# An encoder of two layers in exact fp32 halves: another order of the products in the FFN's second down-projection, and one weight load ordered behind rotary swaps

## The chip, the cores and the metric

The kernel runs on one core of a Trainium2 chip. The metric is the device time of one execution in microseconds (us), the median of several runs. The engines are named as the profile names them: PE is TensorE (matmuls; PEld its weight loads), DVE is VectorE, ACT is ScalarE, POOL is GpSimd, and SP is SyncE, which here issues DMAs and nothing else. "SPq" is SP's queue.

## The reference

Two layers of an encoder over 512 tokens of width 1024, all in fp32:

```python
for i in range(DEPTH):                       # 2 layers
    h = rmsnorm(x, norm_mix[i])
    qa, ka, va, glu_in, qc, kc, vc, gates = split(h @ w_in[i])
    ya = diff_attention(qa, ka, va, ...)     # 4 heads, q and k rotated (rope)
    yb = conformer_conv(glu_in, ...)         # 31 taps, depthwise
    yc = neighbourhood_attention(qc, kc, vc, rpb[i])
    ga, gb, gc = split(sigmoid(gates))
    x = x + (ga*(ya @ w_br_a) + gb*(yb @ w_br_b) + gc*(yc @ w_br_c)) @ w_o[i]
    h = rmsnorm(x, norm_ffn[i])
    x = x + (silu(h @ w_ffn_gate[i]) * (h @ w_ffn_up[i])) @ w_ffn_down[i]   # 1024 -> 2816 -> 1024
    h = rmsnorm(x, norm_ple[i])
    x = x + sigmoid(h @ w_ple_gate[i]) * (p[i] @ w_ple_in[i])
return rmsnorm(x, norm_final)
```

The rotation of q and k is `x * cos + rot * sin`, where `rot` holds the two halves of each head's 64 rows exchanged.

## The kernel before

**Halves.** Every fp32 operand of a product is split into a high half, which ACT writes (a Copy into fp32r, L150), and a low half, which DVE writes (the operand less the high half, L164). Each product of 128 rows is then three matmuls: high by high, high by low, low by high. The loader `weights` (from L172) loads a weight block of up to 128x1024 on SP (L178) into one of three buffers `wr` and splits it into `wh` (ACT) and `wl` (DVE), of which there are three each too. Loads and splits get a higher priority, so that the scheduler places them ahead of the place where the program writes them.

**Who orders what.** PE executes in the order in which the program is written. On ACT, DVE, POOL and SP a scheduler sets the order of instructions by priorities and by what they wait for, before the program runs. An explicit edge without a wait, `behind(i, then)`, tells that scheduler to place `i` behind `then`.

**Differential heads.** `diff_in` (from L836) does one head: for q and then for k a projection (whose weight load is that of `weights`), a copy of the result to `rp`, four swaps of 32 rows each from one `rp` buffer to another by DMA on SP (L852, "rotary swaps"), then on DVE the two products with the tables, their sum and the split, and four or more DMAs that stack the halves (L670). In the profile a swap is `diff_rp<-diff_rp`, the products with the tables end in `diff_rp<-diff_rp,diff_r`, and the names' numbers tell tiles apart: `diff_rp_1483` is filled by the swaps of k of head 0, and `diff_wr_1930` is the weight load of q of head 2. The neighbourhood attention (`natten_...`) and the convolution (`conv_...`) of the same layer run among this work; `diff_mm` at L185 is the first matmul of the next projection.

**FFN.** Its 22 blocks of 128 hidden rows are done in three parts, of 8, 7 and 7 blocks. Within a part `seven` (from L1126) does gate and up of a block with seven products instead of eight, in the manner of Strassen (L1168 to L1170). After the first and the second part `seven_down` (from L1024) adds what the part's hidden rows give to the output, for four pairs p = 0 to 3 of output blocks of 128 rows. A pair takes seven products R0, R1, T0, T1, A0, A1, C0, and the whole-weight products M and N for the part's last chunk:

```python
steps = dict(R0=(R, 0, "a11", "b11"), R1=(R, 1, "s2", "t1"), T0=(T, 0, "s3", "t2"),
             T1=(T, 1, "s1", "t3"), A0=(A, 0, "a12", "b21"), A1=(A, 1, "s4", "b22"),
             C0=(C, 0, "a22", "t4"))
```

Each step names its PSUM tile and half, its weight operand and its activation operand. A product is 9 matmuls of 128x256 (L1068 to L1070); M and N together are the matmuls of 128x512 (L1079 to L1081). The weight operands a11, a12, m0 come from one load; s1, s2, m1 are sums, which the DMAs form as they land in a `qk` tile (loads on SP at L1033 to L1035, added to by POOL's DMAs at L1039); the third and the fourth sum are made by DVE from the others: s3 = s1 + a22, s4 = s3 + a12. Then the two pairs of sums are split: ffn_wh and ffn_wl hold s1, s2, m1; ffn_y (pair 2) or ffn_pt (pair 3) hold both halves of s3 and s4. So DVE's last work for a pair before PE can take T0's low half is the `TENSOR_TENSOR` to ffn_y or ffn_pt. When R0 and R1 are done, ACT copies R; when R and T are complete, DVE takes four subtractions and then the two additions whose results go out by DMA on SP (L1121, `xa`).

The order in which a pair's steps stand in the program is a string. It differs by pair and by `last`, which is 1 in the second part. In the second part, pair 1 has T0 seventh of nine steps (M and N are steps here), pair 2 third and pair 3 second. In pair 2 R and T are the `sc` tiles of PSUM and A is `av`; in pair 3 R and T are the `tr` tiles and A and C `mm`. After pair 3 of the second part comes the third part's first block, whose loads for the blocks ahead (L1133 to L1138) are among the pair's own on SP.

## Time and profile before

| | us |
| --- | --- |
| median of 3 runs | 1765.66 |
| lowest and highest run | 1763.92, 1765.74 |
| the profiled execution | 1766.5 |
| its span, first to last instruction | 1764.7 |
| PE busy in the span | 1753.3 (99%) |
| DVE busy | 1474.0 (84%) |
| ACT busy | 929.3 (53%) |
| POOL busy | 140.3 (8%) |

The profile lists for each engine the instructions with their start and length. An idle time before an instruction stands in square brackets, followed by what ended it: "[0.88 <-DVE ffn_y L164]" is 0.88 us in which the engine waited for a DVE instruction of line 164 that wrote ffn_y. The granted TensorE clock over the profiled execution was 0.999 of full speed. PE's records are shown longer than the distance between two of their starts, because matmuls are pipelined; lengths of stages are therefore read from start to start. In all there are 10578 matmuls in the trace.

### The profile page before, as it was taken

What the parts mean: (1) busy time and instruction counts of PE and PEld (TensorE: products, weight loads), DVE (VectorE), ACT (ScalarE), POOL (GpSimd) and SP (SyncE); (2) the same over time, 40 slices, a digit from 0 to 9 for tenths busy, and PEclk for the clock granted to TensorE, in tenths of its full rate; (3) what the DMA queues carried; (4) which work ended last, traced back from release to release, by engine and by line L of the source; (5) the groups of instructions that cost most, each with busy time, mean ns of one, the idle gap of its engine ahead of it and who ended that gap; (6) DMA issues with size and microseconds to landing.
All of it is one profiled execution on the core that took longest, in us unless ns stands there. A gap on an engine that the chain in (4) does not pass through costs nothing.

```text
span 1764.7 us, 28718 instructions
## 1 busy us (share of the span) xinstructions
PE 1753.3 (99%) x10578; PEld 1565.9 (89%) x10578; DVE 1474.0 (84%) x2528; ACT 929.3 (53%) x1623; POOL 140.3 (8%) x162
## 2 busy tenths in 40 slices
PE   9999999999999999999999999999999999999998
PEld 7888888888899999998888888888888999999987
DVE  7967987998799889887777678889887997988786
ACT  5576545225576455454545655553356654545454
POOL 0000000000111111210000000000001121212100
PEclk9999999999999999999999999999999999999999
DMA  6576641334867777975546755323358668679642
GB/s 225 164 185 160 162 126 44 112 99 140 264 166 174 203 195 174 252 195 164 164 134 172 183 150 152 111 72 96 97 178 241 177 167 223 175 197 241 160 153 95
DMA packets 137901, 288.67 MB, mean 164 GB/s; under 512 B 17184, under 2 KB 38432, under 8 KB 137760
## 3 DMA queue, kind: packets, MB, share of 16 engines
q1 hardware_dynamic: 117456, 251.96, 46.7%
q0 software_dynamic: 19584, 33.56, 11.9%
q8 instruction: 83, 1.36, 0.3%
q10 hardware_dynamic: 720, 1.31, 0.2%
q14 instruction: 58, 0.48, 0.1%
HBM read 236.43 MB, written 19.92 MB: 145 GB/s over the span
## 4 chain that ended last, share of the span: by engine, by line
PE 90%; DVE 5%; ACT 3%; DMA 1%; issue 1%; SPq 0%; POOLq 0%; DVEq 0%; ACTq 0%
PE ffn_mm L1168 4%; PE ffn_mm L1170 4%; PE ffn_mm L1169 4%; PE ffn_sc L1168 3%; PE ffn_sc L1170 3%; PE ffn_sc L1169 3%; PE mergea_mm L187 2%; PE mergea_mm L186 2%; PE mergea_mm L185 2%; PE gateb_mm L186 2%; PE gateb_mm L187 2%; PE wo_mm L186 2%; PE wo_mm L185 2%; PE gateb_mm L185 2%; PE wo_mm L187 2%; PE diff_sc L834 2%
## 5 line engine op out<-in xcount | busy, mean ns | idle before, releaser
L167 DVE SCALAR_TENSOR_TENSOR conv_z<-glu_z,pre_par,conv_z 128x512 f32<-128x512 f32 x240 | 179.4, 748 | 3.4
L1138 POOL DMA_DIRECT2D ffn_qk<-w_fu x88 | 77.7, 964 | 437.3 <-DMA ffn_qk<-w_fu 131.5
L164 DVE TENSOR_TENSOR ffn_wl<-ffn_wr,ffn_wh 128x1024 fp32r<-128x1024 f32 (+1 forms) x76 | 89.3, 1177 | 6.7 <-ACT ffn_wh L150 6.7
L150 ACT ACTIVATE ffn_wh<-ffn_qk 128x1024 fp32r<-128x1024 f32 (+1 forms) x60 | 62.7, 1046 | 49.5 <-PE ffn_mm L1081 14.6
L150 ACT ACTIVATE ffn_wh<-ffn_wr 128x1024 fp32r<-128x1024 f32 (+1 forms) x76 | 76.9, 1014 | 22.5 <-PE ffn_mm L186 12.0
L164 DVE TENSOR_TENSOR ffn_wl<-ffn_qk,ffn_wh 128x1024 fp32r<-128x1024 f32 (+1 forms) x60 | 72.3, 1205 | 8.2 <-ACT ffn_wh L150 7.9
L150 ACT ACTIVATE mergea_wh<-mergea_wr 128x1024 fp32r<-128x1024 f32 (+1 forms) x32 | 27.1, 846 | 96.8 <-PE mergea_mm L186 79.6
L150 ACT ACTIVATE ffn_kh<-ffn_r 128x512 fp32r<-128x512 f32 (+1 forms) x60 | 35.9, 598 | 39.4 <-PE ffn_mm L1169 19.9
L231 POOL TENSOR_TENSOR diff_rc<-diff_sm,pre_power 128x4 f32<-128x4 f32 x8 | 8.9, 1116 | 564.4 <-DVE diff_sm L167 505.9
L150 ACT ACTIVATE natten_e<-natten_e,natten_s 128x192 f32<-128x192 f32 (+1 forms) x88 | 39.3, 473 | 26.2 <-DVE natten_s L732 22.9
L150 ACT ACTIVATE diff_a<-diff_sc,diff_s 128x512 f32<-128x512 f32 x32 | 22.0, 686 | 56.7 <-DVE diff_s L925 56.6
L1168 PE MATMUL ffn_sc<-wo_h,ffn_wh 128*128 128x256 f32 x176 | 50.4, 287 | 0.2 <-ACT ffn_t L150 0.2
L1169 PE MATMUL ffn_mm<-wo_h,ffn_wh 128*128 128x256 f32 x176 | 49.8, 283 | 0.0
L1170 PE MATMUL ffn_mm<-wo_h,ffn_wl 128*128 128x256 f32 x176 | 49.8, 283 | 0.0
L1168 PE MATMUL ffn_mm<-wo_h,ffn_wh 128*128 128x256 f32 x176 | 49.8, 283 | 0.0
L1170 PE MATMUL ffn_sc<-wo_h,ffn_wl 128*128 128x256 f32 x176 | 49.8, 283 | 0.0
L1169 PE MATMUL ffn_sc<-wo_h,ffn_wh 128*128 128x256 f32 x176 | 49.8, 283 | 0.0
L164 DVE TENSOR_TENSOR diff_wl<-diff_wr,diff_wh 128x1024 fp32r<-128x1024 f32 x24 | 29.4, 1223 | 18.6 <-ACT diff_wh L150 13.6
L150 ACT ACTIVATE natten_wh<-natten_wr 128x1024 fp32r<-128x1024 f32 x24 | 25.4, 1058 | 36.7 <-issue 15.2
L925 DVE TENSOR_REDUCE diff_s<-diff_sc 128x1 f32<-128x512 f32 x64 | 42.0, 682 | 2.2 <-PE diff_sc L834 2.1
L164 DVE TENSOR_TENSOR natten_wl<-natten_wr,natten_wh 128x1024 fp32r<-128x1024 f32 x24 | 29.3, 1222 | 12.4 <-ACT natten_wh L150 10.4
L164 DVE TENSOR_TENSOR ffn_qk<-ffn_qk,ffn_r 128x512 f32<-128x512 f32 (+1 forms) x60 | 38.8, 647 | 0.0
(1082 smaller groups left out, 6980.2 us busy)
## 6 DMA issues: line engine op xcount, KB each, us to landing
ffn_qk<-w_fu POOLq DMA_DIRECT2D x88, 256.0 KB, 6.2
ffn_wr<-w_fg SPq DMA_DIRECT2D x44, 512.0 KB, 5.6
ffn_r<-w_fu SPq DMA_DIRECT2D x44, 256.0 KB, 3.7
ffn_qk<-w_fg SPq DMA_DIRECT2D x44, 256.0 KB, 4.7
ffn_qk<-w_fu SPq DMA_DIRECT2D x44, 256.0 KB, 5.1
ffn_wr<-w_fd SPq DMA_DIRECT2D x24, 448.0 KB, 4.2
natten_wr<-w_in SPq DMA_DIRECT2D x16, 512.0 KB, 4.6
diff_wr<-w_in SPq DMA_DIRECT2D x16, 512.0 KB, 4.2
```

The lines of the kernel that those rows point to most:

```text
L150: i = self.nc.scalar.activation(out, in_, func, **kw)
L164: return self.nc.vector.tensor_tensor(out, a, b, op)
L167: return self.nc.vector.scalar_tensor_tensor(out, a, s, b, op0, op1)
L185: mm(out, wh, ah, start=first, stop=False, skip_group_check=onto)
L186: mm(out, wh, al, start=False, stop=False, skip_group_check=onto)
L187: mm(out, wl, ah, start=False, stop=last, skip_group_check=onto)
L834: self.nc.tensor.matmul(out, st4[:, u, qs], st[:, ks], start=n == 0, stop=n == 1)
L925: nc.vector.tensor_reduce(out=m[:, u:u + 1], in_=sc, op=ALU.max, axis=AX.X, negate=True)
L1138: nc.gpsimd.dma_start(q, wu[:, lo], accum_op=ALU.add)
L1168: mm(out, wh[:, c], bh, start=first and k == 0, stop=False, skip_group_check=True)
L1169: mm(out, wh[:, c], bl, start=False, stop=False, skip_group_check=True)
L1170: mm(out, wl[:, c], bh, start=False, stop=k == 3, skip_group_check=True)
```

## The change

Two edits. The first is one condition and one string, in the order of the steps in the second part's down-projection: pair 2's order string is changed and now holds for pair 3 too, which had the default order. Within it the products of the third sum (T0) and of the fourth sum (A1) stand fifth and eighth of nine; before, T0 was third in pair 2 and second in pair 3, and A1 was eighth in both. The second edit adds an ordering edge on SP: the weight load of head 2's q (`s` = 0) is placed behind the last swap of head 0's k.

```diff
@@ weights
-            self.nc.sync.dma_start(raw[:, :n], ap[:, :n])
+            load = self.nc.sync.dma_start(raw[:, :n], ap[:, :n])
+            if self.hold is not None:
+                self.behind(load, self.hold)
@@ build
+        self.hold = None
@@ diff_in
         for s, off in enumerate((OFF_QA, OFF_KA)):
+            self.hold = self.swap if (head, s) == (2, 0) else None
             ps = self.proj(off + head * P)
             ...
             for b in range(4):
                 o = b ^ 1
-                self.nc.sync.dma_start(rot[32 * b:32 * b + 32], raw[32 * o:32 * o + 32])
+                swap = self.nc.sync.dma_start(rot[32 * b:32 * b + 32], raw[32 * o:32 * o + 32])
             ...
+        if head == 0:
+            self.swap = swap
@@ seven_down
         order = "R0 T0 R1 T1 A0 M N A1 C0"
         ...
-        elif last and p == 2:
-            order = "R0 A0 T0 R1 T1 M N A1 C0"
+        elif last:
+            order = "R0 A0 R1 T1 T0 M N A1 C0"
```

Line numbers of the changed kernel are 2 higher past L178, 3 higher past `build`, 4 higher at the swaps and 6 higher in `seven_down`. The next rows are PE's, layer 0, second part, pair 2: the first matmul of each product, before. `ffn_v` to `ffn_x` are activation operands, `ffn_sc_7507` is R, `ffn_sc_7508` is T, `ffn_av_7509` is A; `ffn_y_4772` holds the high half of s3 and s4.

```order
L1068 MATMUL ffn_sc_7507<-ffn_v_4774,ffn_wh_7491 128x256
...
L1068 MATMUL ffn_av_7509<-ffn_v_4775,ffn_wh_7491 128x256
...
L1068 MATMUL ffn_sc_7508<-wo_h_4414,ffn_y_4772 128x256
...
L1068 MATMUL ffn_sc_7507<-ffn_x_4783,ffn_wh_7499 128x256
...
L1068 MATMUL ffn_sc_7508<-ffn_x_4783,ffn_wh_7499 128x256
...
L1079 MATMUL ffn_av_7509<-ffn_y_4780,ffn_wh_7491 128x512
```

And the same place of PE after the change:

```order
L1074 MATMUL ffn_sc_7507<-ffn_v_4774,ffn_wh_7491 128x256
...
L1074 MATMUL ffn_av_7509<-ffn_v_4775,ffn_wh_7491 128x256
...
L1074 MATMUL ffn_sc_7507<-ffn_x_4783,ffn_wh_7499 128x256
...
L1074 MATMUL ffn_sc_7508<-ffn_x_4783,ffn_wh_7499 128x256
...
L1074 MATMUL ffn_sc_7508<-wo_h_4414,ffn_y_4772 128x256
...
L1085 MATMUL ffn_av_7509<-ffn_y_4780,ffn_wh_7491 128x512
```

The product that reads `ffn_y_4772` moved from the third to the fifth place, behind the two that read `ffn_wh_7499`; M, N, A1 and C0 stand where they stood. In pair 3 the same holds with the tiles `ffn_tr_7617`, `ffn_tr_7618` and `ffn_pt_4770`.

The second place is SP in layer 0, around head 0's swaps, before:

```order
L178 DMA gatec_wr_1865<-w_in 128x1024
L852 DMA diff_rp_1403<-diff_rp_1402 32x512 x4
L716 DMA natten_e_1656<-bias 128x448
L852 DMA diff_rp_1483<-diff_rp_1482 32x512
L178 DMA diff_wr_1930<-w_in 128x1024
L852 DMA diff_rp_1483<-diff_rp_1482 32x512 x3
L670 DMA diff_qk_1322<-diff_kh_1413 64x512 x2
L670 DMA diff_qk_1322<-diff_rp_1402 64x512 x2
```

And after:

```order
L178 DMA gatec_wr_1865<-w_in 128x1024
L856 DMA diff_rp_1403<-diff_rp_1402 32x512 x4
L719 DMA natten_e_1656<-bias 128x448
L856 DMA diff_rp_1483<-diff_rp_1482 32x512 x4
L178 DMA diff_wr_1930<-w_in 128x1024
L673 DMA diff_qk_1322<-diff_kh_1413 64x512 x2
L673 DMA diff_qk_1322<-diff_rp_1402 64x512 x2
```

The load of 128x1024 stood between the first and the second of the k swaps and now stands behind the fourth.

The third place is SP at the end of pair 3 in layer 0, where the third part's loads and the outputs of the down-projection (`xa`) mix, before. `ffn_wr_7966` and `ffn_wr_8099` are gate weights of the third and the fourth block of the third part, `ffn_r` holds up weights, and the two loads to `ffn_qk_4788` are the sums of the fourth block:

```order
L1135 DMA ffn_wr_7966<-w_fg 128x1024
L1121 DMA xa_67<-ffn_t_7559 128x512
L1121 DMA xa_67<-ffn_t_7547 128x512
L1136 DMA ffn_r_7967<-w_fu 128x512
L1135 DMA ffn_wr_8099<-w_fg 128x1024
L1133 DMA ffn_qk_4788<-w_fg 128x512
L1134 DMA ffn_qk_4788<-w_fu 128x512
L1121 DMA xa_67<-ffn_t_7660 128x512
```

And after:

```order
L1141 DMA ffn_wr_7966<-w_fg 128x1024
L1127 DMA xa_67<-ffn_t_7559 128x512
L1127 DMA xa_67<-ffn_t_7538 128x512
L1142 DMA ffn_r_7967<-w_fu 128x512
L1139 DMA ffn_qk_4788<-w_fg 128x512
L1140 DMA ffn_qk_4788<-w_fu 128x512
L1141 DMA ffn_wr_8099<-w_fg 128x1024
L1127 DMA xa_67<-ffn_t_7669 128x512
```

The load of `ffn_wr_8099` stood ahead of the two loads of sums and now stands behind them. On DVE, in the same place, the split to ffn_wl of the third part's first block stands two places earlier, and the split to ffn_y of the same block one place later.

## The prediction

> **What bounds the kernel now.** I read the page's busy times first, then the waits of TensorE (PE), then a table of stages around them, then the timelines of the engines they name.

> ```profile
> PE 1753.3 (99%) x10578; PEld 1565.9 (89%) x10578; DVE 1474.0 (84%) x2528; ACT 929.3 (53%) x1623; POOL 140.3 (8%) x162
> ```

> PE is busy in 99% of the span, in the order in which its program is written: only PE work removed or a wait of PE removed can shorten the kernel. The change removes no product, so everything hangs on waits. PE's waits, with columns total us, count, longest:

> ```profile
> PE ffn_sc L1070 <- DVE ffn_y L164: 1.8, 2, 0.9
> PE ffn_tr L1070 <- DVE ffn_pt L164: 1.1, 2, 0.5
> PE diff_mm L185 <- DVE natten_y L164: 0.8, 1, 0.8
> ```

> The first two sit in the down-projections after the FFN's second part, once per layer: PE waits for the low half of the third and fourth sums (ffn_y in pair 2, ffn_pt in pair 3), which DVE writes. The third is one wait in layer 0's attention stage. The next table cuts the second part's down-projections into pair 1, pair 2 and pair 3 (first three rows layer 0, last three layer 1), from each pair's first product to the next one's; columns are length, then busy us of PE, PEld, DVE, ACT, POOL with instruction counts, granted clock, DMA share, GB/s.

> ```profile
> 695.73:704.67 8.94, 8.94 (x72) 8.68 (x71) 7.88 (x13) 4.05 (x6) 1.76 (x2) 1.00 0.85 213
> 704.67:714.78 10.11, 9.23 (x72) 8.77 (x70) 7.25 (x15) 3.88 (x6) 1.73 (x2) 1.00 0.97 276
> 714.78:724.51 9.73, 9.20 (x72) 8.74 (x71) 8.27 (x14) 4.55 (x6) 1.72 (x2) 1.00 0.90 250
> 1568.77:1577.70 8.93, 8.93 (x71) 8.67 (x70) 7.87 (x13) 4.06 (x6) 1.75 (x2) 1.00 0.85 215
> 1577.70:1587.81 10.11, 9.23 (x71) 8.77 (x70) 7.26 (x15) 3.88 (x6) 1.76 (x2) 1.00 0.98 273
> 1587.81:1597.54 9.73, 9.20 (x72) 8.74 (x71) 8.27 (x14) 4.56 (x6) 1.72 (x2) 1.00 0.95 260
> ```

> A pair is the same 72 matmuls each time, at the same clock of 1.00. Pair 1, which already takes its third sum late, needs 8.94 and 8.93 us; pair 2 needs 10.11 and pair 3 9.73.

> **The change: order of the products.** It removes and adds no instruction; the excess of pairs 2 and 3 over pair 1 is the most that a better order can return. Layer 0: (10.11 - 8.94) + (9.73 - 8.94) = 1.96. Layer 1: (10.11 - 8.93) + (9.73 - 8.93) = 1.98. Together **3.94 us**. Whether all of it comes back depends on when the low halves are written:

> ```profile
> 704.67 0.28 PE L1068 MATMUL ffn_sc<-ffn_v,ffn_wh 128*128 128x256 f32 x1
> ...
> 705.75 0.28 PE L1068 MATMUL ffn_av<-ffn_v,ffn_wh 128*128 128x256 f32 x1
> ...
> 708.14 0.39 PE L1070 MATMUL ffn_sc<-wo_h,ffn_y 128*128 128x256 f32 x1 [0.88 <-DVE ffn_y L164]
> ...
> 699.96 1.08 DVE L164 TENSOR_TENSOR ffn_wl<-ffn_qk,ffn_wh 128x896 fp32r<-128x896 f32 x1
> ...
> 707.14 0.95 DVE L164 TENSOR_TENSOR ffn_y<-ffn_qk,ffn_y 128x768 fp32r<-128x768 f32 x1
> ```

> Pair 2: a product takes 705.75 - 704.67 = 1.08 us. The changed order puts T0, the only early user of ffn_y, fifth: it starts at 704.67 + 4 x 1.08 = 708.99, and its third matmul, which reads the low half, at about 709.23. DVE has written that at 707.14 + 0.95 = 708.09, so 1.1 us are left over, and pair 2's wait goes whole. R1, now third at 706.83, reads first and second sums whose low half was done at 699.96 + 1.08 = 701.04: 5.8 us to spare. T1 reads the same tile.

> ```profile
> 716.79 0.39 PE L1070 MATMUL ffn_tr<-wo_h,ffn_pt 128*128 128x256 f32 x1 [0.53 <-DVE ffn_pt L164]
> ...
> 712.18 0.96 ACT L150 ACTIVATE ffn_wh<-ffn_qk 128x896 fp32r<-128x896 f32 x1 [1.23 <-PE ffn_av L1081]
> ...
> 713.17 1.09 DVE L164 TENSOR_TENSOR ffn_wl<-ffn_qk,ffn_wh 128x896 fp32r<-128x896 f32 x1
> ...
> 715.78 0.95 DVE L164 TENSOR_TENSOR ffn_pt<-ffn_qk,ffn_pt 128x768 fp32r<-128x768 f32 x1
> ```

> Pair 3 now starts 1.17 us earlier, at 713.61; do its operands come earlier too? ACT's 712.18 split waited for PE, for the end of pair 2's whole-weight products (L1081), which release the weight buffer. Those stand sixth in pair 2 before and after, so they end 1.17 earlier, and the splits at 712.18, 713.17 and 715.78 move with them. That gives: R1, third from 713.61, at 715.77 against its low half at 713.17 + 1.09 - 1.17 = 713.09 (2.7 to spare); T0, fifth, its third matmul at 717.93 + 0.24 = 718.17 against 715.78 + 0.95 - 1.17 = 715.56 (2.6 to spare). Had nothing moved with PE, the margins would be 1.5 and 1.4; still no wait. So pair 3's goes too.

> What is late next is the third part, which PE reaches 1.96 us earlier:

> ```profile
> 720.16 0.42 DVE L164 TENSOR_TENSOR ffn_a<-ffn_tr,ffn_t 128x256 f32<-128x256 f32 x1 [1.43 <-PE ffn_tr L1070]
> ...
> 723.01 1.23 DVE L164 TENSOR_TENSOR ffn_wl<-ffn_qk,ffn_wh 128x1024 fp32r<-128x1024 f32 x1
> ...
> 721.91 1.06 ACT L150 ACTIVATE ffn_wh<-ffn_qk 128x1024 fp32r<-128x1024 f32 x1 [2.31 <-PE ffn_mm L1081]
> ...
> 727.37 0.28 PE L1168 MATMUL ffn_sc<-wo_rp,ffn_wh 128*128 128x256 f32 x1
> ```

> DVE's subtraction at 720.16 waits for pair 3's T. T was complete after four products and is now complete after five, so relative to PE it is 1.08 later: 720.16 - 1.96 + 1.08 = 719.28. The DVE queue behind it therefore moves up by only 0.88. Behind it stands the low half at 723.01, done by 723.01 + 1.23 - 0.88 = 723.36; PE asks for it at the third matmul of the product of 727.37, 727.37 + 0.24 - 1.96 = 725.65: 2.3 us to spare. ACT's split ahead of it waited 2.31 for PE (the buffer again), not for a load, so it moves with PE. I take no wait here.

> A price is due on SyncE's queue (SP), where the gate load of the third part's fourth block (ffn_wr_8099) now stands behind that block's two loads of sums:

> ```profile
> 722.74 0.33 SPq L1135 DMA_DIRECT2D ffn_wr<-w_fg  x1
> ...
> 742.80 1.05 ACT L150 ACTIVATE ffn_wh<-ffn_wr 128x1024 fp32r<-128x1024 f32 x1
> ...
> ffn_wr<-w_fg SPq DMA_DIRECT2D x44, 512.0 KB, 5.6
> ```

> It is issued at 722.74, lands 5.6 us later by the median of such loads, at 728.3, and ACT first reads it at 742.80. The two loads ahead take some 0.3 us each to issue and may have to wait for their buffers; there are 742.80 - 728.3 - 2 = 12.5 us for that. Taken at nothing; with the cover gone it costs at most one landing, 5.6 us a layer.

> **The change: the held load.** SP sends four swaps of 32 rows per rotary operand. In layer 0, one k swap of head 0 was issued, then a 512 KB weight load, then the other three; the rows below are SP's issues, followed by issue to landing of the three groups, and by the wait in the chain that ended last:

> ```profile
> 144.08 0.51 SPq L852 DMA_DIRECT2D diff_rp<-diff_rp  x1
> ...
> 144.68 0.53 SPq L178 DMA_DIRECT2D diff_wr<-w_in  x1
> ...
> 145.26 1.77 SPq L852 DMA_DIRECT2D diff_rp<-diff_rp  x3
> ...
> diff_rp<-diff_rp SPq DMA_DIRECT2D x1, 64.0 KB, 2.3
> ...
> diff_wr<-w_in SPq DMA_DIRECT2D x1, 512.0 KB, 6.4
> ...
> diff_rp<-diff_rp SPq DMA_DIRECT2D x3, 64.0 KB, 5.7
> ...
> 146.45 5.25 DMA diff_rp<-diff_rp
> ...
> 151.81 0.69 DVE L164 TENSOR_TENSOR diff_rp<-diff_rp,diff_r 128x512 f32<-128x512 f32 x1 [1.99 <-DMA diff_rp<-diff_rp]
> ...
> 157.82 0.68 DVE L164 TENSOR_TENSOR natten_y<-natten_y,natten_mm 64x512 fp32r<-64x512 f32 x1
> ...
> 157.55 0.28 PE L728 MATMUL natten_sc<-natten_x,natten_qk 128*128 128x192 f32 x1
> ...
> 158.65 0.47 PE L185 MATMUL diff_mm<-glu_h,diff_wh 128*128 128x512 f32 x1 [0.82 <-DVE natten_y L164]
> ```

> The swap ahead of the load lands in 2.3 us, the three behind it in 5.7. DVE stands idle 1.99 us at 151.81 for them, and what DVE does later, at 157.82, is what PE waits for at 158.65. With all four swaps ahead, the last is issued at about 144.08 + 4 x 0.55 = 146.3 and by the 2.3 of the free swap lands at 148.6, ahead of DVE's readiness at 151.81 - 1.99 = 149.82. So DVE's whole 1.99 goes, natten_y is done at 158.50 - 1.99 = 156.5, and PE, ready at about 157.6, doesn't wait. PE's gap from start to start there is 158.65 - 157.55 = 1.10, of which a step of this form takes 0.12 undisturbed (the spacing of the 0.28 us matmuls within a product, 1.08 / 9); with a little for the wider operand I take **1.05 us** as gain. [...]

> The load's own cost: issued 1.7 us later, it lands by about 144.68 + 6.4 + 1.7 = 152.8. Its reader and the weight's twin in layer 1:

> ```profile
> 167.58 1.05 ACT L150 ACTIVATE diff_wh<-diff_wr 128x1024 fp32r<-128x1024 f32 x1
> ...
> 1024.81 0.69 DVE L164 TENSOR_TENSOR diff_rp<-diff_rp,diff_r 128x512 f32<-128x512 f32 x1 [0.17 <-DMA diff_rp<-diff_rp]
> ...
> 176.27 1.15 PE natten_mm L769 x8
> ```

> ACT reads it at 167.58: 14.8 us of cover, cost nothing; without that cover, up to 6.4. In layer 1 the same swaps cost DVE 0.17 only; I count **0.17**, between nothing and 0.17.

> Sum: 3.94 + 1.05 + 0.17 = **5.16 us**. The profiled execution took 1766.5 us (span 1764.7), so 1761.3; it lay 0.84 above the median of 1765.66, and against that median I predict **1760.5**.

> The other reading of the same waits is by idle rows alone: 1.8 + 1.1 + 0.8 = 3.7 us. I take start to start, since the same 72 matmuls are compared. [...] By idle rows the sum would end at 1762.0.

> **The rivals.**
> - *The held load returns nothing.* The chain runs on behind the removed wait to PE's natten_mm at 176.27; if something else sets that step, PE gives the 1.05 back there, or the swaps land as late as before because other loads share the engines. For it: DVE work between is mostly back to back. Against: DVE's lead of 2 us shifts every link. Result: 3.94 alone, 1761.7.
> - *The wait moves on into the third part.* The DMA share in pairs 2 and 3 is 0.90 to 0.98; if that stage were fed by loads, PE arriving 1.96 earlier would wait there. Against: both ACT splits name PE as releaser. Result: only 1.05 + 0.17, 1764.4.
> - *Pair 3's wait stays,* because its splits are set by loads after all and DVE order shifts against it: 0.79 + 0.80 = 1.59 less, 1762.1.
> - *Slower: the gate load that moved.* If the two loads of sums ahead of it wait for buffers more than 12.5 us, SP holds it and every load behind, and PE waits one landing in each layer: 2 x 5.6 = 11.2, less 5.16: +6.0, 1771.7. It decides from 12.5 us on; the longest hold among the SP rows above is the 1.77 of three swaps.

> **How the numbers follow.** About 0.2%, 3.5 us, is what a measurement of this kernel can tell from no change; the line lies at 1762.1. Chances: forecast 0.65, no return from the load 0.13 (1761.7), wait moves on 0.10 (1764.4), pair 3 stays 0.08 (1762.1), slower 0.04 (1771.7). The three runs span 1.8 us, so a case has that much play: the forecast lands below the line in nearly all of its share (0.61), the second in two thirds (0.09), pair 3 in half (0.04): faster 0.74. Same 0.22, slower 0.04. The range goes down by the play of 1.9 to 1758.6; up past 1761.7, 1762.0 and 1762.1 with their play to 1763.8, leaving out most of the moved wait and the slower case.

> **What would show it.** Right: pairs 2 and 3 at about 8.95 us each, no ffn_y or ffn_pt among PE's waits, no new wait of L1168 past pair 3; SP issues four swaps in a row, DVE's wait at 151.81 gone, diff_mm 0.2 behind its forerunner. Wrong: a wait of PE for ffn_wl in the third part, SP held ahead of the moved gate load, swaps that still land more than 4 us after issue, or a PE wait at natten_mm grown by as much as was gained.

## The result, and the profile after

The changed kernel takes 1760.41 us (median of 8 runs, 1759.68 to 1761.55), the kernel before 1765.94 us over its 8 runs: ratio 0.9971, 95% interval 0.996 to 0.9982. The forecast was 1760.5, with a range of 1758.6 to 1763.8. The profiled execution took 1761.55 us, its span is 1759.8, against 1764.7 before.

PE's waits after the change, in the columns shown for before (total, count, longest):

```profile
PE pre_av L338 <- DVE pre_zeror L411: 1.1, 1, 1.1
PE natten_mm L772 <- DVE natten_a L164: 0.3, 1, 0.3
PE natten_av L772 <- DVE natten_a L164: 0.3, 1, 0.3
PE ffn_sc L1174 <- ACT ffn_t L150: 0.2, 1, 0.2
```

The three waits on which the prediction was built are gone: ffn_y (1.8), ffn_pt (1.1) and natten_y at diff_mm (0.8). One that wasn't there before stands in second place: 0.3 at natten_mm, in layer 1. The second part's pairs 1, 2 and 3, layer 0 and then layer 1, from start to start:

```profile
694.36:703.29 8.93, 8.93 (x71) 8.67 (x70) 7.87 (x13) 4.05 (x6) 1.76 (x2) 1.00 0.80 209
703.29:712.23 8.94, 8.94 (x71) 8.68 (x70) 7.26 (x15) 3.88 (x6) 1.74 (x2) 1.00 1.03 288
712.23:721.17 8.94, 8.94 (x71) 8.68 (x70) 7.19 (x12) 3.97 (x5) 1.75 (x2) 1.00 0.99 271
1566.16:1575.10 8.94, 8.94 (x72) 8.68 (x70) 7.88 (x13) 4.06 (x6) 1.75 (x2) 1.00 0.83 215
1575.10:1584.04 8.94, 8.94 (x72) 8.68 (x70) 7.26 (x15) 3.89 (x6) 1.76 (x2) 1.00 0.93 277
1584.04:1592.98 8.94, 8.94 (x72) 8.68 (x70) 7.18 (x12) 3.96 (x5) 1.75 (x2) 1.00 0.99 266
```

Pairs 2 and 3 now take what pair 1 takes, 8.94 us, with PE busy throughout. The FFN term is (10.11 - 8.94) + (9.73 - 8.94) = 1.96 in each layer, 3.92 us. The margins behind it, and the gate load that moved on SP:

```profile
705.77 0.95 DVE L164 TENSOR_TENSOR ffn_y<-ffn_qk,ffn_y 128x768 fp32r<-128x768 f32 x1
...
707.61 0.28 PE L1074 MATMUL ffn_sc<-wo_h,ffn_y 128*128 128x256 f32 x1
...
719.78 1.22 DVE L164 TENSOR_TENSOR ffn_wl<-ffn_qk,ffn_wh 128x1024 fp32r<-128x1024 f32 x1
...
722.39 0.38 SPq L1141 DMA_DIRECT2D ffn_wr<-w_fg  x1
...
739.47 1.04 ACT L150 ACTIVATE ffn_wh<-ffn_wr 128x1024 fp32r<-128x1024 f32 x1
```

In pair 2 the low half is written at 706.72 and T0's third matmul stands at 707.61 + 0.24 = 707.85: 1.13 us to spare, where 1.1 were forecast. The third part's ffn_wl is done at 721.00, and PE takes it at 724.27: 3.3 us to spare, where 2.3 were forecast, since the scheduler placed that split two places earlier on DVE. The gate load is issued at 722.39 and read at 739.47, 17 us later: the cover is there.

In layer 0's heads (SP, then DVE, then PE):

```profile
144.04 2.41 SPq L856 DMA_DIRECT2D diff_rp<-diff_rp  x4
146.54 0.53 SPq L178 DMA_DIRECT2D diff_wr<-w_in  x1
...
149.85 0.68 DVE L164 TENSOR_TENSOR diff_rp<-diff_rp,diff_r 128x512 f32<-128x512 f32 x1
...
155.84 0.68 DVE L164 TENSOR_TENSOR natten_y<-natten_y,natten_mm 64x512 fp32r<-64x512 f32 x1
...
157.62 0.41 PE L187 MATMUL diff_mm<-glu_h,diff_wh 128*128 128x512 f32 x1
...
174.94 0.98 PE L772 MATMUL natten_mm<-natten_pt,natten_v 128*128 128x256 f32 x6
```

DVE's step that came at 151.81 after 1.99 us of waiting comes at 149.85 with none, natten_y at 155.84 instead of 157.82, and diff_mm at 157.62 instead of 158.65. At natten_mm, where a rival expected the time back, PE is further ahead: 174.94 against 176.27, 1.33 us. Layer 1's heads give a part of it back:

```profile
1017.44 0.69 DVE L164 TENSOR_TENSOR diff_rp<-diff_rp,diff_r 128x512 f32<-128x512 f32 x1 [1.87 <-DMA diff_rp<-diff_rp]
...
1020.83 0.44 PE L772 MATMUL natten_mm<-natten_a,natten_x 128*128 128x128 f32 x2 [0.34 <-DVE natten_a L164]
```

This wait of DVE is for head 0's q swaps, ahead of everything that the edit moves in that layer; it was 1.08 before. Followed along PE's starts the two traces differ by 1.33 after layer 0's heads, 3.34 after its FFN (724.51 against 721.17), 2.60 after layer 1's heads (a matmul of diff_sc at 1057.25 is now at 1054.65) and 4.56 after its FFN (1597.54 against 1592.98). So 1.33 + 2.01 - 0.74 + 1.96 = 4.56; the rest of the 4.9 between the spans lies behind PE's last matmul.

### The profile page after: what moved, and what is told of

It reads as the page before. It is cut to its first block, busy times and chain, and to the rows that moved or that the text cites. A ratio compares the mean times of both kernels' runs of the same rounds, so it can differ in the third digit from the quotient of the medians.

```text
span 1759.8 us, 28716 instructions
## 1 busy us (share of the span) xinstructions
PE 1752.0 (100%) x10578; PEld 1565.5 (89%) x10578; DVE 1473.8 (84%) x2528; ACT 929.6 (53%) x1623; POOL 140.3 (8%) x162
## 3 DMA queue, kind: packets, MB, share of 16 engines
q8 instruction: 83, 1.36, 0.3%
q10 hardware_dynamic: 720, 1.31, 0.2%
## 4 chain that ended last, share of the span: by engine, by line
PE 92%; DVE 4%; ACT 2%; DMA 1%; issue 1%; SPq 0%; POOL 0%; ACTq 0%; POOLq 0%; DVEq 0%
PE ffn_mm L1174 4%; PE ffn_mm L1176 4%; PE ffn_mm L1175 4%; PE ffn_sc L1174 3%; PE ffn_sc L1176 3%; PE ffn_sc L1175 3%; PE mergea_mm L188 2%; PE mergea_mm L189 2%; PE mergea_mm L187 2%; PE gateb_mm L188 2%; PE gateb_mm L189 2%; PE gateb_mm L187 2%; PE wo_mm L187 2%; PE wo_mm L189 2%; PE wo_mm L188 2%; PE diff_sc L837 2%
## 5 line engine op out<-in xcount | busy, mean ns | idle before, releaser
L164 DVE TENSOR_TENSOR ffn_wl<-ffn_wr,ffn_wh 128x1024 fp32r<-128x1024 f32 (+1 forms) x76 | 89.3, 1177 | 6.7 <-ACT ffn_wh L150 6.7
L150 ACT ACTIVATE ffn_wh<-ffn_qk 128x1024 fp32r<-128x1024 f32 (+1 forms) x60 | 62.7, 1045 | 51.8 <-PE ffn_mm L1087 14.6
L150 ACT ACTIVATE ffn_wh<-ffn_wr 128x1024 fp32r<-128x1024 f32 (+1 forms) x76 | 76.8, 1014 | 22.5 <-PE ffn_mm L188 12.0
L150 ACT ACTIVATE mergea_wh<-mergea_wr 128x1024 fp32r<-128x1024 f32 (+1 forms) x32 | 27.1, 846 | 96.8 <-PE mergea_mm L188 79.6
L164 DVE TENSOR_TENSOR ffn_wl<-ffn_qk,ffn_wh 128x1024 fp32r<-128x1024 f32 (+1 forms) x60 | 72.3, 1205 | 6.7 <-ACT ffn_wh L150 6.3
L150 ACT ACTIVATE ffn_kh<-ffn_r 128x512 fp32r<-128x512 f32 (+1 forms) x60 | 35.9, 599 | 42.0 <-PE ffn_mm L1175 19.9
L150 ACT ACTIVATE diff_a<-diff_sc,diff_s 128x512 f32<-128x512 f32 x32 | 22.0, 686 | 57.2 <-DVE diff_s L931 57.1
L150 ACT ACTIVATE natten_e<-natten_e,natten_s 128x192 f32<-128x192 f32 (+1 forms) x88 | 39.3, 473 | 24.0 <-DVE natten_s L735 20.7
L164 DVE TENSOR_TENSOR diff_wl<-diff_wr,diff_wh 128x1024 fp32r<-128x1024 f32 x24 | 29.3, 1223 | 18.6 <-ACT diff_wh L150 13.6
L150 ACT ACTIVATE natten_wh<-natten_wr 128x1024 fp32r<-128x1024 f32 x24 | 25.4, 1059 | 36.7 <-issue 15.2
L164 DVE TENSOR_TENSOR natten_wl<-natten_wr,natten_wh 128x1024 fp32r<-128x1024 f32 x24 | 29.3, 1222 | 12.4 <-ACT natten_wh L150 10.4
L164 DVE TENSOR_TENSOR ffn_qk<-ffn_qk,ffn_r 128x512 f32<-128x512 f32 (+1 forms) x60 | 38.9, 648 | 0.0
## 6 DMA issues: line engine op xcount, KB each, us to landing
ffn_wr<-w_fg SPq DMA_DIRECT2D x44, 512.0 KB, 5.5
natten_wr<-w_in SPq DMA_DIRECT2D x16, 512.0 KB, 4.5
diff_wr<-w_in SPq DMA_DIRECT2D x16, 512.0 KB, 4.2
```

Source lines behind the costliest of these rows:

```text
L150: i = self.nc.scalar.activation(out, in_, func, **kw)
L164: return self.nc.vector.tensor_tensor(out, a, b, op)
```

## The experiments

The theory was that the two edits remove separate waits and add up, with theory A's addition that the 0.74 us lost in layer 1 come from the load held there. In single traces PE's opening alone differs by up to 1.1 us between executions (the pre_mm that starts at 9.03 before starts at 8.21 with the load alone and at 9.29 with the products alone), so differences are read at the places concerned, and the totals from the medians.

**The products alone.** The hold is taken out:

```diff
-            self.hold = self.swap if (head, s) == (2, 0) else None
```

> The new order of the products alone; the weight load stands among the swaps again, in both layers. Theory A (the two edits add up, and the 0.7 us that layer 1's heads lost in the changed kernel come from the held load there): the FFN returns 1.96 to 1.98 us per layer, 3.9 in all, so 1762.0 us beside 1765.9 before; PE's wait of 0.8 at diff_mm is back, and no wait of 0.3 at layer 1's natten_mm. Rival B (that loss comes from loads that meet the swaps at another moment once PE is ahead, whatever the order on SP): the same 0.7 us is lost here too, 1762.7.

1762.2 us, ratio 0.9981 (0.9972 to 0.999): 3.4 us by the ratio, 3.6 by the medians. From the list of PE's waits, and DVE in layer 1:

```profile
PE diff_mm L187 <- DVE natten_y L164: 0.7, 1, 0.7
...
PE natten_mm L772 <- DVE natten_a L164: 0.3, 1, 0.3
```

```profile
1018.91 0.69 DVE L164 TENSOR_TENSOR diff_rp<-diff_rp,diff_r 128x512 f32<-128x512 f32 x1 [1.82 <-DMA diff_rp<-diff_rp]
```

The wait in layer 0 is back, as expected. But the 0.3 at natten_mm is here too, with no load held (0.55 us from start to start): theory A's addition falls, and rival B is right that the loss comes without the hold.

**The load alone.** The old order of the products:

```diff
-        elif last:
-            order = "R0 A0 R1 T1 T0 M N A1 C0"
+        elif last and p == 2:
+            order = "R0 A0 T0 R1 T1 M N A1 C0"
```

> The held load alone, both layers; the products stand in the old order. Theory A: layer 0's heads return 1.3 us, layer 1's lose 0.7, so 0.6 us, 1765.3. The prediction's own terms: 1.05 + 0.17 = 1.2, 1764.7. Rival B: 1.3 and nothing lost in layer 1, 1764.6. Rival C (PE gives the time back at the next wait): 1765.9.

1763.95 us, ratio 0.9991 (0.9982 to 1.0): 1.6 us by the ratio, 1.9 by the medians. The two FFN waits are what they were; DVE's wait for layer 1's q swaps is short:

```profile
PE ffn_sc L1076 <- DVE ffn_y L164: 1.8, 2, 0.9
PE ffn_tr L1076 <- DVE ffn_pt L164: 1.1, 2, 0.5
```

```profile
1017.99 0.69 DVE L164 TENSOR_TENSOR diff_rp<-diff_rp,diff_r 128x512 f32<-128x512 f32 x1 [1.18 <-DMA diff_rp<-diff_rp]
```

Layer 1 has no wait at natten_mm, although its load is held. The median lies below all four times that were expected, by 0.6 us and more; the interval (0 to 3.2 us) reaches three of them, and rival C's at its edge. In the trace layer 0's heads return 1.3 us by PE's starts and nothing is given back behind them, so rival C falls as well. The edits add up as far as the runs can tell: 3.4 + 1.6 = 5.0 by the ratios, each with some 1.6 us of play to either side, and 5.1 (0.29% of 1765.94) measured together.

**The hold in layer 0 alone.**

```diff
-            self.hold = self.swap if (head, s) == (2, 0) else None
+            self.hold = self.swap if (self.i, head, s) == (0, 2, 0) else None
```

> Both edits, the hold in layer 0 alone. Theory A: layer 1 no longer loses 0.7 us, so 1759.7, and DVE waits about 1.1 us (not 1.9) for layer 1's q swaps. Rival B: the loss stays, 1760.4, and the wait stays near 1.9.

1760.75 us, ratio 0.9974 (0.9965 to 0.9984): no faster than with both. In layer 1, SP around the q swaps and the first k swap, then DVE and PE:

```profile
1011.03 2.45 SPq L856 DMA_DIRECT2D diff_rp<-diff_rp  x4
1013.58 1.91 SPq L719 DMA_DIRECT2D natten_e<-bias  x1
1015.59 0.51 SPq L856 DMA_DIRECT2D diff_rp<-diff_rp  x1
...
1016.44 0.69 DVE L164 TENSOR_TENSOR diff_rp<-diff_rp,diff_r 128x512 f32<-128x512 f32 x1 [1.20 <-DMA diff_rp<-diff_rp]
...
1022.45 0.69 DVE L164 TENSOR_TENSOR diff_rp<-diff_rp,diff_r 128x512 f32<-128x512 f32 x1 [1.35 <-DMA diff_rp<-diff_rp]
...
1029.28 0.47 PE L187 MATMUL diff_mm<-ple_h,diff_wh 128*128 128x512 f32 x1 [1.31 <-DVE natten_y L164]
```

The wait for the q swaps is 1.20, as theory A had it, but its gain didn't come. The k swaps behind the load are late in layer 1 too, by 1.35 us on DVE and 1.31 on PE. Before, the same place cost DVE 0.17; in the run of the products alone it cost nothing. What differs is when SP issued them: its issue of natten_e took 1.91 us here and 0.53 before, so the first k swap went out 4.56 us after the first q swap instead of 3.18. Two traces below have the same delay on SP with the load held in layer 1 (T0 last, 4.69 us, and Twice the bytes, 4.62), and DVE doesn't wait there. So without the hold layer 1's price was 0 to 1.35 us in three traces; with it none of seven shows one.

**Pair 2 alone in the new order.**

```diff
-        elif last:
+        elif last and p == 2:
             order = "R0 A0 R1 T1 T0 M N A1 C0"
```

> Both edits, but pair 3 keeps its default order with T0 second. Theory A (pair 3's operands move with PE, since ACT's split waits for PE's release of the weight buffer): pair 2 returns 1.17 us a layer, pair 3's wait keeps its size of 0.5 by the idle rows and its 9.73 us from start to start, so 1760.4 + 1.6 = 1762.0. Rival (the operands are set by loads or by DVE's own queue and don't move): PE stands in pair 3 for 1.2 us longer, 10.9 us, and 1760.4 + 3.9 = 1764.3.

1761.68 us, ratio 0.9977 (0.9968 to 0.9986): theory A had 1762.0, and the rival's 1764.3 falls. Pairs 2 and 3 in layer 0, and pair 3's wait:

```profile
702.89:711.84 8.95, 8.95 (x72) 8.69 (x71) 7.27 (x15) 3.89 (x6) 1.73 (x2) 1.00 0.99 281
711.84:721.57 9.73, 9.20 (x72) 8.74 (x71) 8.27 (x14) 4.55 (x6) 1.76 (x2) 1.00 0.92 250
```

```profile
713.85 0.39 PE L1076 MATMUL ffn_tr<-wo_h,ffn_pt 128*128 128x256 f32 x1 [0.53 <-DVE ffn_pt L164]
```

Pair 3 takes 9.73 us, to the hundredth what it took before, though PE reaches it earlier: its operands move with PE, as the prediction's working of pair 3 had it.

**T0 fourth.**

```diff
-            order = "R0 A0 R1 T1 T0 M N A1 C0"
+            order = "R0 A0 R1 T0 T1 M N A1 C0"
```

> The changed kernel with T0 fourth instead of fifth in pairs 2 and 3. In the changed kernel's trace ffn_y's low half is done at 705.77 + 0.95 = 706.72, and T0's third matmul stands at 707.61 + 0.24 = 707.85; one product earlier it stands at 706.77. Theory A (only the moment at which T0 meets its low half counts): 0.05 us left in pair 2, 1.5 in pair 3, so no wait or one of some hundredths, 1760.4 to 1760.6. Rival (the low half has to be there well ahead of its matmul): a wait in pair 2 of up to 0.9 in each layer, 1761 to 1762.2.

1760.79 us, ratio 0.9967 (0.9955 to 0.998). Pairs 2 and 3 of layer 0, then DVE and PE in pair 2:

```profile
703.11:712.16 9.05, 9.05 (x72) 8.75 (x71) 7.26 (x15) 3.90 (x6) 1.73 (x2) 1.00 0.99 283
712.16:721.09 8.93, 8.93 (x71) 8.67 (x70) 7.17 (x12) 3.96 (x5) 1.75 (x2) 1.00 0.96 264
```

```profile
705.58 0.95 DVE L164 TENSOR_TENSOR ffn_y<-ffn_qk,ffn_y 128x768 fp32r<-128x768 f32 x1
...
706.59 0.39 PE L1076 MATMUL ffn_sc<-wo_h,ffn_y 128*128 128x256 f32 x1
```

The low half is done at 706.53 and its matmul starts at 706.59. Pair 2 takes 0.11 us longer than with T0 fifth, and pair 3 nothing: the place where the wait ends is where the rows put it.

**T0 last.**

```diff
-            order = "R0 A0 R1 T1 T0 M N A1 C0"
+            order = "R0 A0 R1 T1 M N A1 C0 T0"
```

> The changed kernel with T0 last in pairs 2 and 3. DVE then stands before the subtraction that needs T until the pair's end, with the next sums and their split behind it. Theory A: the split to ffn_pt is done some 4.5 us after pair 2's end, at 717, ahead of A1's third matmul at 718.2, and the third part's a22 low half some 1.0 us after pair 3's end, 0.4 ahead of its matmul: no wait, 1760.4, so the order has room on both sides. Rival (T's lateness is what the order has to avoid): PE waits in the third part for ffn_a or ffn_y, 0.5 to 2 us in each layer, 1761.4 to 1764.4.

1760.92 us, ratio 0.9968 (0.9956 to 0.9981). Pairs 2 and 3 in layer 0:

```profile
703.57:712.51 8.94, 8.94 (x71) 8.68 (x70) 6.22 (x10) 4.50 (x6) 1.74 (x2) 1.00 0.93 284
712.51:721.45 8.94, 8.94 (x71) 8.68 (x70) 7.35 (x12) 4.09 (x5) 1.72 (x2) 1.00 0.95 231
```

No wait in either pair, and no new one in the third part. At the fifth place and at the ninth there is none, so the order has room; lateness of T costs nothing here.

**Twice the bytes ahead of the swaps.** In layer 0, a transfer of 1 MB behind the first of head 0's k swaps, the other three behind it:

```diff
+                if (self.i, head, s) == (0, 0, 1):
+                    if b:
+                        self.behind(swap, more)
+                    else:
+                        flat = self.xp[0:4].rearrange("k p n -> (k p) n")
+                        more = self.nc.sync.dma_start(
+                            flat.rearrange("(q r) n -> q (r n)", r=2),
+                            self.a["w_in"][0, 0:2].rearrange("a p n -> (a p) n"))
+                        self.behind(more, swap)
```

> The changed kernel with one more transfer of 1 MB, twice the load's bytes, between the first and the second of head 0's k swaps, in layer 0 alone; nothing reads what it writes. Theory A (a swap lands behind the bytes ahead of it on the queue): the load of 512 KB put the last swap at 151.69 instead of 149.44, 2.25 us; 1 MB puts it 4.5 later, at 153.9; DVE, free at 149.82, waits 4.1 us and PE at diff_mm 0.94 less than that, 3.2 us, 1763.6. Rival (the delay came with that load's buffer or place, not with its bytes): 1760.4.

1763.14 us, ratio 0.9983 (0.9974 to 0.9992): above the changed kernel by 2.1 us by the ratios, by 2.7 by the medians. DVE and PE, then the table of stages behind the wait:

```profile
152.67 0.69 DVE L164 TENSOR_TENSOR diff_rp<-diff_rp,diff_r 128x512 f32<-128x512 f32 x1 [3.51 <-DMA diff_rp<-diff_rp]
...
157.05 0.28 PE L731 MATMUL natten_sc<-natten_x,natten_qk 128*128 128x192 f32 x1
159.49 0.76 PE L187 MATMUL diff_mm<-glu_h,diff_wh 128*128 128x512 f32 x1 [2.17 <-DVE natten_y L164]
160.06 0.63 PE L188 MATMUL diff_mm<-glu_h,diff_wh 128*128 128x512 f32 x1
```

```profile
159.40:161.00 1.60, 1.51 (x4) 1.25 (x5) 1.04 (x3) 1.57 (x5) 0.00 (x0) 0.50 0.24 56
161.00:162.60 1.60, 1.60 (x5) 1.23 (x4) 1.35 (x4) 1.27 (x4) 0.00 (x0) 0.50 0.86 199
162.60:165.00 2.40, 2.40 (x16) 2.06 (x15) 1.70 (x9) 1.56 (x7) 0.00 (x0) 1.00 0.85 199
```

The swaps are late behind another transfer too, with another target, so that load's buffer isn't the cause: theory A holds in its direction. Its proportion doesn't: DVE waits 3.51 us (4.1 expected), PE 2.17 (3.2 expected), and 512 KB had cost DVE 1.99. The swaps land right behind the transfer in front of them (landings at 151.05 for the 512 KB and 151.31 to 151.69 for the swaps; 151.59 for the 1 MB and 151.90 to 152.55 for the swaps), and 1 MB took 7.5 us from issue to landing where 512 KB took 6.4. A second cost follows the wait: in the table's first two rows PE's granted clock is 0.50.

**One more load held.** The first gate load behind head 0's q swaps, in both layers:

```diff
+            if (head, s) == (0, 0):
+                self.swapq = swap
@@ gate_c
+        self.hold = self.swapq if m == 0 else None
         ps = self.proj(OFF_G + 2 * D + m * P)
+        self.hold = None
```

> The changed kernel with one more load held: the first gate load of 512 KB, which stands ahead of head 0's q swaps, behind the last of these, in both layers. Theory A: the q swaps land some 1 to 2 us earlier, DVE's wait for them in layer 1 (1.87 in the changed kernel's trace, 1.1 to 1.3 in others) goes, and with it PE's 0.34 at natten_mm where there was one: 1759.9 to 1760.4. Rival (the gate load's landing becomes late): ACT reads it 14 us after its landing now, so a loss would show as a wait of ACT at gatec_wh, up to 4.5 us, 1761 or more.

1761.34 us, ratio 0.9973 (0.9963 to 0.9984): not faster. DVE and PE in layer 1:

```profile
1016.04 0.69 DVE L164 TENSOR_TENSOR diff_rp<-diff_rp,diff_r 128x512 f32<-128x512 f32 x1 [2.02 <-DMA diff_rp<-diff_rp]
...
1017.91 0.68 DVE L164 TENSOR_TENSOR natten_pt<-natten_tr,natten_pt 128x512 fp32r<-128x512 f32 x1
...
1019.45 0.67 DVE L164 TENSOR_TENSOR natten_y<-natten_av,natten_y 64x512 fp32r<-64x512 f32 x1
...
1021.22 0.44 PE L772 MATMUL natten_mm<-natten_a,natten_x 128*128 128x128 f32 x2 [1.01 <-DVE natten_a L164]
```

Both expectations missed. The step that needs the swaps does come earlier (1016.04 against 1017.44), and yet DVE waits longer for it: the scheduler placed it ahead of the splits to natten_pt and natten_y. In the changed kernel the split to natten_y ran at 1014.29, before that step; now both stand behind the wait, at 1017.91 and 1019.45, and PE's wait at natten_mm grows from 0.34 to 1.01. The q swaps themselves did land earlier: the last one 4.91 us after the first was issued, against 5.95 in the changed kernel, but DVE was ready for them 1.2 us earlier still.

## Why the prediction was right

- **The bound.** PE's waits set the time, and the three that were named were the ones that the change removed.
- **Products.** 3.94 forecast, 1.96 + 1.96 = 3.92 in the trace, 3.4 by the ratio of the run with the products alone, whose interval (1.8 to 4.9 us) holds both. The margin of 1.1 us in pair 2 measured 1.13, and one product less brought back 0.11 us. That pair 3's operands move with PE was shown by the run with pair 2 alone; with T0 last the third part had room even for a T later than forecast.
- **The held load, layer 0.** 1.05 forecast, 1.33 in the trace: 1.03 at diff_mm, 0.06 in the matmuls right behind, and 0.23 at natten_mm, where the prediction had expected at best no loss. It had overlooked that the freed DVE, through ACT's copy to diff_rp, also feeds that step. The swaps landed in time for DVE at 149.82, so its step starts at 149.85 without a wait, but with less to spare than forecast: the last one landed at 149.44, not at 148.6. A transfer of 16 KB on the queue that the DMA view calls `instruction` ran from 147.06 to 148.01, and the last four packets of the swaps followed one another right behind it, when all others had ended by 147.55. The load issued behind the four swaps, at 146.54, landed at 151.07, after all four.
- **The held load, layer 1.** This term was mis-sized, and its bounds of 0 and 0.17 were taken from one execution. It also took a wait of DVE for one of PE: before, PE stood idle for 0.01 us at layer 1's diff_mm, and from start to start it gained 0.07 there in the changed kernel, 0.10 with the products alone, where nothing is held. Unheld, the three traces show DVE waiting 0.17, 0 and 1.35 us. Held, none. In the runs' medians it can't be seen: 1760.75 without it, 1760.41 with it.
- **What the sum lacked.** In layer 1 PE lost 0.74 us that no term foresaw, of which 0.60 from start to start, 0.34 by the idle row, is lost at natten_mm. The runs put it on the q swaps: DVE waited 1.87 us for them in the changed kernel and PE lost 0.60 there; 1.82 and 0.55 with the products alone, 1.52 and 0.26 with T0 fourth, 1.36 and 0.09 with T0 last; with 1.26 or less (five traces, the kernel before among them) PE lost nothing. What DVE waits beyond some 1.27 us is lost one to one, whichever edit is in. The run with the gate load held, in another order on DVE, had 2.02 and PE's wait.
- **Why the q swaps are late.** The traces point to one thing, though no run moves it. In layer 1 one 16 KB transfer of the queue `instruction` runs among the q swaps in all ten traces, and the last swap lands 1.2 to 1.6 us after it ends. DVE is ready 4.2 us after the first swap's issue in nine of them; the transfer ended 4.5 and 4.6 us after that issue in the two traces with the longest waits, and 3.7 to 4.2 in the other seven. Layer 0 has no such transfer among its q swaps, and DVE waits 0.5 us at most for them in the same nine. Why it runs later in some executions is open, and so is the share of the gate load in front, which was held in a run that changed DVE's order too.
- **Rivals.** The wait that moves into the third part, pair 3's wait that stays and a loss from the gate load that moved are all absent from the trace. That the load returns nothing is excluded by the trace; by time alone its interval (0 to 3.2 us) only just allows it.

The total came out within 0.1 us of the forecast, which is better than its terms deserve: layer 0's heads gave 0.28 more and layer 1's took 0.9 more (0.74 lost where 0.17 was to be won) in the profiled execution, and the runs themselves span 1.9 us. Luck is in the base as well: the forecast was a fall of 5.16 us from 1765.66, the median of three runs; measured against the median of eight the fall is 5.5, by the ratio 5.1 (3.2 to 7.1).

## What to carry to other kernels

Where one engine is busy 99% of the span, list its waits, find a stage of the same work that has none, and take the difference from start to start: that is the gain to be had, and the rows of the producer say at which place in the order the wait ends. Small transfers that the next step needs should not be issued behind a large load that nothing needs for 15 us: here the swap ahead of the 512 KB landed 2.3 us after its issue, the three behind it 5.7. Tell a scheduler of one order and look at all engines' orders afterwards, since it may move the consumer forward and queue other work behind a wait.

## What the runs showed of the hardware

```profile
155.78:159.19 3.41, 1.54 (x14) 1.37 (x12) 3.32 (x11) 2.88 (x11) 0.00 (x0) 1.00 0.54 154
159.19:162.60 3.41, 3.11 (x7) 2.48 (x8) 2.55 (x6) 3.06 (x8) 0.00 (x0) 0.50 0.52 120
...
1752.37:1755.78 3.41, 1.76 (x16) 1.52 (x15) 2.68 (x9) 1.34 (x3) 0.74 (x2) 1.00 0.14 52
1755.78:1759.19 3.41, 0.00 (x0) 0.00 (x0) 0.47 (x2) 0.27 (x1) 0.00 (x0) 1.00 0.69 258
```

  A stretch with PE busy for 45% was followed by half the clock, one with 52% was not; at the end of the trace the clock fell after a stretch with 27% in the kernel before (1757.70 to 1761.11, 0.93 us busy) and after an idle one in the changed kernel (1754.17 to 1757.59). The last row above is idle for 3.41 us, longer than the gap of 2.4, and still at full clock, so in these traces it isn't the length of a gap alone that counts. That it is how much of one such stretch the gap fills is the author's reading of these few cases and was not tested.
- Swaps of 64 KB issued behind a 512 KB load landed right behind it (0.3 to 0.6 us in layer 0 before). In layer 1 the last of them landed 5.9 to 6.8 us after the first was issued in the three unheld traces, and cost DVE 0 to 1.35 us: 1.35 where the first k swap went out 4.56 us after the first q swap, 0.17 where it was 3.18.
- One transfer of 16 KB on the queue `instruction` (147.06 to 148.01) ran while swaps were under way: in layer 0 of the changed kernel the last two landed at 149.19 and 149.44, 2.5 us and more behind the second (146.65). That it held them up, and that the q swaps of layer 1 are late for the same reason, is read from ten traces and not tested.
